# A two-layer chunk-banded attention step on one core: layer B's gates projected with the weights held still, and the softmax sums divided into the probabilities

## The chip, the cores and the metric

The program runs on one core of one Trainium2 chip. The metric is the device time of one execution in microseconds. The kernel before was run three times: median 2267.89 us, lowest 2266.09, highest 2268.76. One further execution was taken with the hardware profiler, and every view of the trace below is of that one.

## What is computed

Two layers of gated attention run over 2048 prompt tokens and 64 sample tokens, model width 1024. The part of the reference that matters here:

```python
def gated_attention_layer(x_p, x_s, ck, cv, norm_g, w_in, q_g, k_g, w_out, ...):
    qp, kp, vp, gp = project(x_p, norm_g, w_in, q_g, k_g, n_heads, n_kv)
    op = prompt_band_attention(qp, kp, vp, past_chunks, bias_fn, sinks)
    y_p = x_p + (op * jax.nn.silu(gp)) @ w_out
```

`project` normalises each token (RMS over 1024), multiplies with one matrix for queries, keys, values and gates, and normalises each head of the queries and keys again. Layer A has 16 query heads over 2 key heads and a window of 128 tokens; layer B has 16 heads of 64 columns with keys of their own and sees its own chunk of 64 tokens and the 8 chunks before. In layer B the probabilities are a plain softmax, `p = exp(s - m) / sum`, the output of a head is `p @ v`, and it is multiplied by `silu(gate)` before the output matrix.

## The kernel before

All products are made in two parts: a tensor is split into a high and a low float32r part, and a product is the sum of three matmuls, high by high, high by low, low by high. TensorE (PE) runs its instructions in the order in which the program is written; the order on ScalarE (ACT), VectorE (DVE), GpSimd (POOL) and on the DMA queue of SyncE (SP) is set by a scheduler.

The work on PE is one long stream. A `Filler` holds all projections as jobs cut in small steps (one step is the three matmuls of one eighth of the model width) and is advanced to a mark between the pieces of the attention; so a projection of a later unit always lies between the scores and the transposes of an earlier one. Layer A's attention comes first, then layer A's output projection as filler, then layer B's attention with its own projections as filler, and at the end what is left of layer B's output projection.

Layer B goes over 8 pairs of heads (`hp`), and for each pair over 8 prompt units of 256 tokens (two tiles of 128) and one sample unit of 64 tokens. For a prompt unit the steps are:

- **Projection** (`project`, lines 489 to 491). For each tile the activations `xx` stand in the array and the 512 columns of weights of the pair move: 128 each of queries, keys, values and gates. That is 8 x 3 matmuls of 512 columns for a tile, 48 for a unit. The result (`pj`, tokens on the partitions) is read by ACT, scaled by the token's inverse norm (`evacuate`, line 512): 384 columns to `pa`, the 128 gate columns to `pb`.
- **Head norms and gate.** DVE and POOL normalise queries and keys (lines 553, 557, 562); ACT makes a tanh of the gates (line 570) and DVE finishes `silu` up to a factor 0.5 (line 571), both for each tile.
- **Queries and keys** (`queries`). PE turns `pa` into `tp`, ACT writes the high parts (lines 1118, 1119), DVE the low parts: two pairs of subtractions and two copies (lines 1123, 1127, 1136).
- **Scores** (`scores`), once for each of the four pairs of tile and head, in the order of the two tiles of one head, then the two of the other. Four matmuls make up to 640 scores per query in `sb` (lines 1174, 1175), DVE adds the bias and takes the extreme in one instruction (line 1178), ACT takes the exponential into `p` and sums it (line 1182). After the last of the four, DVE inverts the four sums at once (line 1188) and POOL multiplies the gates with them into `G` (line 1196).
- **Values** (`values`), one step after its scores: PE transposes `p` (up to five times 128 x 128, line 626), ACT writes the high part `ph` (line 598), DVE the low part `pl` (line 599).
- **Products** (`products`), after the second tile of a head, between and behind the transposes of the next step: `p` by `v` into `o` (line 1264). For the second head of a unit PE also transposes the two tiles of `G` (line 626, `tp<-ident,G`) and ACT copies them, halved, to `gt` (line 1015). `finish_pairs` then adds the parts of `o`, and POOL multiplies with `gt` (line 1026) and stores.

The sample unit goes its own way through `evacuate_sample`, with its gates as tokens on the partitions. A unit's `queries` come in the second of the four steps of the unit before, so the low parts of queries and keys and the scores of the third step meet on DVE. `sb` has two buffers that scores and transposed probabilities share, `p` three, `pj` two.

Of the kernel before, what the change touches and what calls it, by code (L numbers as in the profile page):

```python
# [9 lines left out]
F32 = mybir.dt.float32  # L10
# [40 lines left out]
def hybrid_encoder_kernel(  # L51
# [87 lines left out]
    skew = dr.tile([2, 16, P, VL], F32, tag="skew", name="skew")  # L139

# [332 lines left out]

    def project(tile_, xc, w, C, res, ps=None):
        tt, t0, n = tile_
        ps = ps or psum("pj", 512, 2)
        for k in range(KC):
            wh, wl = weights_of(w, k)
            xh, xl = xc.parts[k // 2]
            if xl is None:  # L480
                if k == 0:
                    nc.tensor.matmul(ps[:, :C], xh[:, k % 2, :], wh, start=True, stop=False)
                nc.tensor.matmul(ps[:n, :C], xh[:, k % 2, :n], wl, start=False, stop=False)
                if k > 0:
                    nc.tensor.matmul(ps[:, :C], xh[:, k % 2, :], wh, start=False, stop=k == KC - 1)
                cost = 2 * C / 2400
            else:
                xh, xl = (a[:, k % 2, t0 : t0 + n] for a in (xh, xl))
                nc.tensor.matmul(ps[:n, :C], xh, wh, start=k == 0, stop=False)  # L489
                nc.tensor.matmul(ps[:n, :C], xh, wl, start=False, stop=False)  # L490
                nc.tensor.matmul(ps[:n, :C], xl, wh, start=False, stop=k == KC - 1)  # L491
                cost = 3 * C / 2400
            if k < KC - 1:
                yield cost
        res.append(ps)
        return cost
# [533 lines left out]
    def layer_b():  # L1030
# [4 lines left out]
        def add_unit(hp, unit):  # L1035
# [7 lines left out]
            def prefetch():  # L1043
                for j in range(NO):
                    assert finished["x1", j] == 2 or j * OT >= u * UT + T
                st.x[hp, u] = x = load_act(x1, u * UT, T, False, T == TS, None, xs[1], hp > 0)
                return x
# [6 lines left out]
            def gen():  # L1054
# [3 lines left out]
                for e, (tt, t0, n) in enumerate(tiles):  # L1058
                    out = []
                    c = yield from project((tt, t0, n), xc, st.w[hp], 512, out)  # L1060
# [11 lines left out]
                    pr = evacuate(1, tt, n, out[0], 512, P, it.gate[:, e])  # L1072
# [3 lines left out]
                    it.todo += head_norm(n, pr[:n, 0:256]) + gate(n, it.gate[:n, e])  # L1076
# [7 lines left out]
                    it.ready = e == len(tiles) - 1  # L1084
                    yield c
# [55 lines left out]
        def scores(it, i, h):  # L1141
# [45 lines left out]
            if c == w - 1:  # L1187
                nc.vector.reciprocal(it.sm[:n, :w], it.sm[:n, :w])
                it.G = G = t("G", [P, 256])
                if u == NU:  # L1190
                    nc.gpsimd.tensor_tensor(
                        G[:, 0:HD], it.gate[:, 0, 0:HD], it.sm[:, 0:1].to_broadcast([P, HD]), op=ALU.mult
                    )
                    return
                for e in range(len(tiles)):
                    nc.gpsimd.tensor_tensor(
                        G[:n, e * P : (e + 1) * P].rearrange("p (h d) -> p h d", d=HD),
                        it.gate[:n, e].rearrange("p (h d) -> p h d", d=HD),
                        it.sm[:n, 2 * e : 2 * e + 2].unsqueeze(2).to_broadcast([n, 2, HD]),
                        op=ALU.mult,  # L1200
                    )
# [51 lines left out]
        def products(it, h):  # L1253
# [18 lines left out]
            def rest():  # L1272
                if h == 1:
                    n = tiles[0][2]
                    GT = psum("tp", 512, 1)
                    for e, (_, t0, _) in enumerate(tiles):
                        transpose(GT[:, t0 : t0 + n], it.G[:n, e * P : (e + 1) * P])
                    gt = gate_t(GT[:, :T].rearrange("p (j s) -> p j s", j=1), T)
# [4 lines left out]
                if h == 1:  # L1283
                    finish_pairs(
                        it.O[:, : 2 * T].rearrange("p (j e s) -> p j e s", j=1, e=2),
                        gt,
# [87 lines left out]
    def block_scales(o):  # L1374
# [4 lines left out]
        sums_to_scales(1, tiles[0], [sums(tt * P, (tt + 1) * P) for tt in tiles], psum("o", 512, 1))  # L1379

# [183 lines left out]
```

## Time and profile before

| what | value |
|---|---|
| median of three runs | 2267.89 us |
| the profiled execution | 2266.69 us, its span 2264.9 us |
| granted TensorE clock | 0.998 |
| busy share of the span: PE, DVE, ACT, POOL | 99%, 69%, 63%, 37% |
| layer B's attention in the span, about | 900 to 2080 us |

The span runs from the first to the last instruction; 1.8 us of the execution lie outside it. Times in the trace are microseconds from the span's start. A row of the timeline gives the start, the duration and the engine, then the line, the operation, the tile written and the tiles read. A matmul's recorded duration holds its whole way through the array, and several are on the way at once; what one of them costs PE in a stream is the distance from its start to the start of the next.

### The profile page before, as it was taken

How to read it: one execution, taken by the hardware profiler on the slowest of the kernel's cores; microseconds unless marked ns; L12 is line 12 of the kernel's file. 1: busy time of each engine (PE TensorE's matmuls, PEld its weight loads, DVE VectorE, ACT ScalarE, POOL GpSimd, SP SyncE). 2: the span in 40 equal slices, each digit the busy share in tenths (PEclk: the TensorE clock that was granted, in tenths of full speed). 3: DMA queues.
4: the chain of work that ended last, by engine and by line, in shares of the span. 5: the costliest groups of instructions: out<-in, count | busy, mean ns of one | idle time of the engine just before them, and what ended most of it. 6: DMA issues, size and time to landing. Idle time of an engine off the chain costs nothing.

```text
span 2264.9 us, 42136 instructions
## 1 busy us (share of the span) xinstructions
PE 2233.4 (99%) x13869; PEld 1965.2 (87%) x13869; DVE 1567.5 (69%) x5184; ACT 1425.0 (63%) x3610; POOL 841.8 (37%) x1196
## 2 busy tenths in 40 slices
PE   8999999999999999999999999999999999999999
PEld 7887888888889998888888888888888888888999
DVE  7889888888785546776776767767767677675211
ACT  6888877777784335766665756656656566566321
POOL 5654533333254456432222322222222222224442
PEclk9999999999999999999999999999999999999999
DMA  8846546754446767454444544544445435444664
GB/s 281 286 137 216 169 140 181 230 175 145 150 133 189 223 194 279 153 192 139 153 144 132 167 136 128 165 144 142 144 138 166 127 120 177 133 128 119 201 184 140
DMA packets 232285, 379.35 MB, mean 167 GB/s; under 512 B 24753, under 2 KB 163393, under 8 KB 232033
## 3 DMA queue, kind: packets, MB, share of 16 engines
q1 hardware_dynamic: 232064, 376.65, 53.8%
q8 instruction: 109, 1.79, 0.3%
q14 instruction: 112, 0.91, 0.1%
HBM read 296.13 MB, written 82.08 MB: 167 GB/s over the span
## 4 chain that ended last, share of the span: by engine, by line
PE 84%; DVE 5%; ACT 5%; issue 3%; DMA 2%; POOL 1%; SPq 0%; ACTq 0%; POOLq 0%; DVEq 0%
PE pj L489 14%; PE pj L491 14%; PE pj L490 14%; PE o L1264 6%; PE sb L626 6%; PE pj L1418 5%; PE pj L1419 4%; PE pj L1420 4%; PE tp L626 3%; PE sb L1175 3%; PE sb L1174 3%; PE sa L626 2%; PE o L971 1%; PE sa L917 1%; PE sa L918 1%
## 5 line engine op out<-in xcount | busy, mean ns | idle before, releaser
L489 PE MATMUL pj<-wh,xx 128*128 128x512 f32 (+1 forms) x1648 | 660.7, 401 | 1.6 <-ACT pb L512 0.9
L490 PE MATMUL pj<-wl,xx 128*128 128x512 f32 (+1 forms) x1648 | 636.5, 386 | 3.1 <-DVE wl L317 3.1
L491 PE MATMUL pj<-wh,xx 128*128 128x512 f32 (+1 forms) x1648 | 637.7, 387 | 0.0
L491 PEld LDWEIGHTS pj<-wh,xx 128*128 128x128 f32 x1648 | 310.2, 188 | 67.6 <-POOL xx L388 0.2
L489 PEld LDWEIGHTS pj<-wh,xx 128*128 128x128 f32 x1648 | 311.0, 189 | 43.1 <-ACT pb L512 1.6
L490 PEld LDWEIGHTS pj<-wl,xx 128*128 128x128 f32 x1648 | 311.5, 189 | 41.4 <-DVE wl L317 3.5
L1182 ACT ACTIVATE p<-p,nm 128x640 f32<-128x640 f32 (+5 forms) x264 | 200.0, 757 | 231.4 <-DVE nm L1178 230.5
L388 POOL TENSOR_TENSOR xx<-xraw,xx 128x528 fp32r<-128x528 f32 (+1 forms) x200 | 266.4, 1355 | 174.8 <-ACT xx L387 155.1
L557 POOL TENSOR_TENSOR f<-f,mhalf 128x4 f32<-128x4 f32 (+3 forms) x221 | 226.8, 1027 | 213.0 <-DVE f L553 204.1
L599 DVE TENSOR_TENSOR pl<-sb,ph 128x640 fp32r<-128x640 f32 (+4 forms) x264 | 193.4, 733 | 151.5 <-ACT ph L598 150.3
L1418 PE MATMUL pj<-xx,wh 128*128 128x264 f32 x1024 | 293.5, 287 | 0.2 <-DVE res L1423 0.2
L1419 PE MATMUL pj<-xx,wh 128*128 128x264 f32 x1024 | 291.4, 285 | 0.2 <-POOL xx L388 0.2
L1420 PE MATMUL pj<-xx,wl 128*128 128x264 f32 x1024 | 289.9, 283 | 0.0
L1178 DVE CUSTOM_DVE_ANT_0 p<-sb,BT 128x640 f32<-128x640 f32 (+5 forms) x272 | 197.0, 724 | 78.1 <-PE sb L1175 66.2
L1026 POOL TENSOR_TENSOR o<-gt,o 128x256 f32<-128x256 f32 (+1 forms) x132 | 103.5, 784 | 376.6 <-ACT p L934 105.5
L626 PE MATMUL sb<-ident,p 128*128 128x128 f32 x1144 | 213.3, 280 | 3.4 <-ACT sq L570 1.1
L387 ACT CAST xx<-xraw 128x528 fp32r<-128x528 f32 (+1 forms) x200 | 121.3, 627 | 142.6 <-PE pj L1420 126.7
L598 ACT CAST ph<-sb 128x640 fp32r<-128x640 f32 (+4 forms) x264 | 162.9, 617 | 63.1 <-PE sb L626 59.5
L1418 PEld LDWEIGHTS pj<-xx,wh 128*128 128x128 f32 x1024 | 192.8, 188 | 0.9 <-DVE res L1423 0.4
L1419 PEld LDWEIGHTS pj<-xx,wh 128*128 128x128 f32 x1024 | 192.4, 188 | 0.6 <-POOL xx L388 0.4
L1420 PEld LDWEIGHTS pj<-xx,wl 128*128 128x128 f32 x1024 | 192.6, 188 | 0.0
L1423 DVE TENSOR_TENSOR res<-pj,res 128x264 f32<-128x264 f32 x128 | 55.0, 430 | 190.7 <-PE pj L1420 184.0
(212 smaller groups left out, 4815.2 us busy)
## 6 DMA issues: line engine op xcount, KB each, us to landing
xx<-xsb SPq DMA_DIRECT2D x224, 512.0 KB, 4.2
xx<-xsa SPq DMA_DIRECT2D x88, 512.0 KB, 4.7
xraw<-oga SPq DMA_DIRECT2D x64, 264.0 KB, 3.5
xraw<-ogb SPq DMA_DIRECT2D x64, 264.0 KB, 3.4
xsa<-xx SPq DMA_DIRECT2D x32, 512.0 KB, 4.4
wraw<-in_w_in_b_dram SPq DMA_DIRECT2D x64, 256.0 KB, 3.1
xsb<-xx SPq DMA_DIRECT2D x32, 512.0 KB, 4.9
xraw<-in_x_dram SPq DMA_DIRECT2D x40, 256.0 KB, 4.0
```

The lines of the kernel that those rows point to most:

```text
L388: nc.gpsimd.tensor_tensor(xl, rv, xh.bitcast(F32), op=ALU.subtract)
L489: nc.tensor.matmul(ps[:n, :C], xh, wh, start=k == 0, stop=False)
L490: nc.tensor.matmul(ps[:n, :C], xh, wl, start=False, stop=False)
L491: nc.tensor.matmul(ps[:n, :C], xl, wh, start=False, stop=k == KC - 1)
L557: nc.gpsimd.tensor_tensor(fv, fv, mhalf[:n, :H], op=ALU.pow)
L599: b = nc.vector.tensor_tensor(dst_lo, src, dst_hi.bitcast(F32), op=ALU.subtract)
L626: nc.tensor.transpose(out, in_, ident[:n, :n])
L1178: mi = nc.vector.tensor_tensor_reduce(out=p[r, :nk], in0=S[r, o : o + nk], in1=b, op0=ALU.add, op1=ALU.min, scale=1.0, scalar=3e38, accum_ ...
L1182: ex = nc.scalar.activation(p[:n, :nk], p[:n, :nk], AF.Exp, scale=-1.0, bias=it.nm[:n, c : c + 1], accum_out=it.sm[:n, c : c + 1],)
L1418: nc.tensor.matmul(ps[:, :OT], wh, oh, start=k == 0, stop=False)
L1419: nc.tensor.matmul(ps[:, :OT], wh, ol, start=False, stop=False)
L1420: nc.tensor.matmul(ps[:, :OT], wl, oh, start=False, stop=k == KC - 1)
```

## The change

Three things change for the prompt units of layer B; layer A and the sample units keep their arithmetic.

1. `project` now makes 384 columns (queries, keys, values) for each tile. The gates come in a third pass over the same weights and activations, `project_turned`: the 128 gate columns of the weights stand in the array and the 256 tokens of the unit move. The result has the gate columns on the partitions and the tokens along the row.
2. In that layout the inverse norm of a token is a number for each column. It is written to DRAM once per tile (`rows_b`), and for each unit spread over the partitions by a DMA (`rb`, 128 KB). DVE multiplies it in while it reads `pj`, ACT makes one tanh of 128 x 256, DVE finishes. `finish_pairs` takes the gates as they are: the transposes of `G`, the copy to `gt` and the products on POOL are gone.
3. The inverse sums go into the probabilities: for each of the four pairs of tile and head DVE inverts one sum, and ACT multiplies `p` by it in place, ahead of the transposes.

```diff
+    def project_turned(xc, w, C, T, res):
+        ps = psum("pj", 512, 2)
+        for k in range(KC):
+            wh, wl = (a[:, C : C + P] for a in weights_of(w, k))
+            xh, xl = (a[:, k % 2, :T] for a in xc.parts[k // 2])
+            nc.tensor.matmul(ps[:, :T], wh, xh, start=k == 0, stop=False)
+            nc.tensor.matmul(ps[:, :T], wh, xl, start=False, stop=False)
+            nc.tensor.matmul(ps[:, :T], wl, xh, start=False, stop=k == KC - 1)
...
@@ layer_b, prefetch
+                if not last:
+                    it.row = t("rb", [P, UT])
+                    load(it.row, rows_b[u].partition_broadcast(P))
@@ layer_b, gen
-                    c = yield from project((tt, t0, n), xc, st.w[hp], 512, out)
+                    c = yield from project((tt, t0, n), xc, st.w[hp], 512 if last else 384, out)
...
-                    pr = evacuate(1, tt, n, out[0], 512, P, it.gate[:, e])
+                    pr = evacuate(1, tt, n, out[0], 384, 0)
...
-                    it.todo += head_norm(n, pr[:n, 0:256]) + gate(n, it.gate[:n, e])
+                    it.todo += head_norm(n, pr[:n, 0:256])
...
+                    c = yield from project_turned(xc, st.w[hp], 384, T, out)
+                    g = it.gate.rearrange("p a b -> p (a b)")
+                    nc.vector.scalar_tensor_tensor(g, out[0][:, :T], 0.5, it.row, op0=ALU.mult, op1=ALU.mult)
+                    e = t("sq", [P, 256], 2)
+                    nc.scalar.activation(e, g, AF.Tanh)
+                    nc.vector.scalar_tensor_tensor(g, e, 1.0, g, op0=ALU.add, op1=ALU.mult)
@@ scores
-            if c == w - 1:
-                nc.vector.reciprocal(it.sm[:n, :w], it.sm[:n, :w])
+            nc.vector.reciprocal(it.sm[:n, c : c + 1], it.sm[:n, c : c + 1])
...
-                for e in range(len(tiles)):
-                    nc.gpsimd.tensor_tensor(
-                        G[:n, e * P : (e + 1) * P].rearrange("p (h d) -> p h d", d=HD),
...
+            else:
+                nc.scalar.activation(p[:n, :nk], p[:n, :nk], AF.Identity, scale=it.sm[:n, c : c + 1])
@@ products
-                if h == 1:
-                    n = tiles[0][2]
-                    GT = psum("tp", 512, 1)
-                    for e, (_, t0, _) in enumerate(tiles):
-                        transpose(GT[:, t0 : t0 + n], it.G[:n, e * P : (e + 1) * P])
-                    gt = gate_t(GT[:, :T].rearrange("p (j s) -> p j s", j=1), T)
...
-                        gt,
+                        it.gate.rearrange("p a b -> p (a b)").unsqueeze(1),
@@ block_scales
+        for tt in tiles:
+            if tt < NT:
+                store(rows_b[tt // 2][tt % 2 * P : (tt % 2 + 1) * P].rearrange("(p o) -> p o", o=1), rr[1][:, tt : tt + 1])
```

Below, the order in which instructions stand on their engines, in the unit with tokens 512 to 767 of the fifth head pair; lines of after are 10 to 40 higher for the same code. First the PE of before where the projection passes from one tile to the next: `pj` is the projection's result, `wh` and `wl` the weights' parts, `xx` the activations, `sb` the scores.

```order
L489 MATMUL pj_19807<-wh_18859,xx_19616 128x512
L490 MATMUL pj_19807<-wl_18860,xx_19616 128x512
L491 MATMUL pj_19807<-wh_18859,xx_19616 128x512
L1174 MATMUL sb_19881<-KA,q_3978_19774 128x384
L1175 MATMUL sb_19881<-KA,q_1_102 128x384
L1174 MATMUL sb_19881<-KA,q_3978_19774 128x256
L1175 MATMUL sb_19881<-KA,q_1_102 128x256
L489 MATMUL pj_19900<-wh_18384,xx_19610 128x512
```

The PE of after where the projection passes from the second tile to the turned pass:

```order
L503 MATMUL pj_20705<-wh_19582,xx_20427 128x384
L504 MATMUL pj_20705<-wl_19583,xx_20427 128x384
L505 MATMUL pj_20705<-wh_19582,xx_20427 128x384
L480 MATMUL pj_20771<-xx_20421,wh_19076 128x256
L481 MATMUL pj_20771<-xx_20421,wh_19076 128x256
L482 MATMUL pj_20771<-xx_20421,wl_19077 128x256
```

A tile's steps move 384 columns in place of 512, and a third result of 8 x 3 steps of 256 columns follows, in which the activations are what moves. Next the PE of before at the products that end a unit: `ident,p` are transposes of probabilities, `ident,G` those of the gates, `o` the products.

```order
L626 MATMUL sb_19936<-ident,p_19882 128x128
L1264 MATMUL o_19855<-ph_19851,VT 128x256
L1264 MATMUL o_19855<-ph_19851,VT 128x128
L626 MATMUL sb_19936<-ident,p_19882 128x128
L1264 MATMUL o_19855<-pl_19852,VT 128x128
L626 MATMUL sb_19936<-ident,p_19882 128x128 x3
L626 MATMUL tp_19947<-ident,G_19842 128x128 x2
L1264 MATMUL o_19855<-pl_19852,VT 128x256
```

The same place of after:

```order
L640 MATMUL sb_20777<-ident,p_20712 128x128
L1283 MATMUL o_20682<-ph_20678,VT 128x256
L1283 MATMUL o_20682<-ph_20678,VT 128x128
L640 MATMUL sb_20777<-ident,p_20712 128x128
L1283 MATMUL o_20682<-pl_20679,VT 128x128
L640 MATMUL sb_20777<-ident,p_20712 128x128 x3
L1283 MATMUL o_20682<-pl_20679,VT 128x256
```

Only the two transposes of `G` are gone. Last the DVE of before behind the third scores of that unit: line 1136 copies and lines 1123 and 1127 make the low parts of the next unit's queries and keys, line 562 ends its head norm, line 599 is the low part of the transposed probabilities of the step before, line 1178 the next bias and extreme.

```order
L1136 CAST q_4018_19980<-q_4018_19980 64x256
L1123 SCALAR_TENSOR_TENSOR q_0_101<-tp_19975,qsc,q_4018_19980 64x256
L1127 SCALAR_TENSOR_TENSOR KA<-tp_19975,ksc,KA 64x256
L562 TENSOR_TENSOR pa_19970<-pa_19970,f_19994 128x256
L599 TENSOR_TENSOR pl_19935<-sb_20020,ph_19934 128x5x128
L1123 SCALAR_TENSOR_TENSOR q_0_101<-tp_19975,qsc,q_4018_19980 64x256
L1127 SCALAR_TENSOR_TENSOR KB<-tp_19975,ksc,KB 64x256
L1136 CAST q_4018_19980<-q_4018_19980 64x256
L571 SCALAR_TENSOR_TENSOR pb_19806<-sq_20031,pb_19806 128x128
L1178 ISA p_20041,nm_19880<-sb_20040,BT 128x640
```

The DVE of after behind the third scores of the same unit, from their own bias and extreme on; line 1107 reads the turned gates, line 1213 inverts a sum:

```order
L1204 ISA p_20831,nm_20710<-sb_20830,BT 128x640
L1204 ISA nm_20710 128x1
L1162 CAST q_3956_20825<-q_3956_20825 64x256 x2
L576 TENSOR_TENSOR pa_20767<-pa_20767,f_20789 128x256
L1107 SCALAR_TENSOR_TENSOR pb_20641<-pj_20771,rb_20429 128x256
L1149 SCALAR_TENSOR_TENSOR q_0_109<-tp_20820,qsc,q_3956_20825 64x256
L1153 SCALAR_TENSOR_TENSOR KA<-tp_20820,ksc,KA 64x256
L1149 SCALAR_TENSOR_TENSOR q_0_109<-tp_20820,qsc,q_3956_20825 64x256
L1153 SCALAR_TENSOR_TENSOR KB<-tp_20820,ksc,KB 64x256
L1213 RECIPROCAL sm_20709<-sm_20709 128x1
L613 TENSOR_TENSOR pl_20776<-sb_20874,ph_20775 128x5x128
L1110 SCALAR_TENSOR_TENSOR pb_20641<-sq_20856,pb_20641 128x256
```

The inversion of the third sum stands behind the copies, the head norm's end, the reading of the turned gates and all four low parts, and the low part of the step before now stands behind it. In 30 heads of full width (640 scores) the inversion stands behind all four low parts, and in 19 of these behind lines 576 and 1107 too.

## Prediction on record

> **What bounds the kernel now.** I read the page first, for the engine that sets the end. Of its chain of waits this is the share by engine:
>
> ```profile
> PE 84%; DVE 5%; ACT 5%; issue 3%; DMA 2%; POOL 1%; SPq 0%; ACTq 0%; POOLq 0%; DVEq 0%
> ```
>
> TensorE carries it. Next the table by stretches over layer B's attention (1060 to 2040 us, five stretches), of which the sum shows whether any other engine is near its limit there; then the table of what PE waited for in 1060 to 2060 us, its two largest entries:
>
> ```profile
> sum 980.00, PE 977.53 PEld 843.86 DVE 698.29 ACT 620.40 POOL 270.29; mean PE 195.51 PEld 168.77 DVE 139.66 ACT 124.08 POOL 54.06
> ```
>
> ```profile
> PE sb L626 <- ACT sq L570: 1.1, 3, 0.4
> PE tp L626 <- ACT gt L1015: 1.1, 1, 1.1
> ```
>
> PE is busy 977.5 of 980 us, and its longest waits sum to about 1 us each; DVE is at 71%, ACT at 63%. So in this stage a microsecond of instructions taken from PE's stream or put into it is a microsecond of the run, and the other engines matter only where they make PE wait. What a matmul costs in the stream is read as the distance between starts, from PE's timeline of two units:
>
> ```profile
> 1701.37 0.39 PE L489 MATMUL pj<-wh,xx 128*128 128x512 f32 x1
> ...
> 1702.52 0.39 PE L491 MATMUL pj<-wh,xx 128*128 128x512 f32 x1
> ...
> 1704.70 0.34 PE L1174 MATMUL sb<-KB,q 128*128 128x384 f32 x1
> 1704.87 0.34 PE L1175 MATMUL sb<-KB,q 128*128 128x384 f32 x1
> 1705.05 0.28 PE L1174 MATMUL sb<-KB,q 128*128 128x256 f32 x1
> 1705.17 0.28 PE L1175 MATMUL sb<-KB,q 128*128 128x256 f32 x1
> 1705.29 0.40 PE L489 MATMUL pj<-wh,xx 128*128 128x512 f32 x1
> ...
> 1707.56 0.29 PE L626 MATMUL sb<-ident,p 128*128 128x128 f32 x1
> 1707.61 0.37 PE L1264 MATMUL o<-pl,VT 128*128 128x256 f32 x1
> ...
> 1716.55 0.30 PE L626 MATMUL sb<-ident,p 128*128 128x128 f32 x1
> 1716.68 0.38 PE L626 MATMUL tp<-ident,G 128*128 128x128 f32 x2
> 1716.82 0.37 PE L1264 MATMUL o<-pl,VT 128*128 128x256 f32 x1
> 1717.02 0.28 PE L1264 MATMUL o<-ph,VT 128*128 128x256 f32 x1
> ...
> 1717.73 0.39 PE L489 MATMUL pj<-wh,xx 128*128 128x512 f32 x1
> ```
>
> Five distances of 512 columns take 1.15 us (1701.37 to 1702.52), so 0.230 to 0.232 us each; two of 384 take 0.35, so 0.175; six of 256 columns 0.71 (1717.02 to 1717.73), so 0.118. From a transpose to the next product are 0.05 us without the gates' transposes (1707.56) and 0.27 us with them (1716.55).
>
> **The change part by part.** There are 64 prompt units (8 head pairs, 8 units); each term is for one, then times 64.
>
> *The projection.* Before: 48 x 0.232 = 11.14 us. After: 48 x 0.175 + 24 x 0.118 = 8.40 + 2.83 = 11.23 us. The columns are the same; 24 more starts cost 0.096 us, times 64 = **+6.1 us**, all on the path. With 0.230 for the wide one and 0.120 (1705.05 to 1705.29) for the narrow it would be +15, with 0.174 and 0.117 +1.5; I take the longer measurements, +6.
>
> *The gates' transposes.* Two leave each unit: 0.27 - 0.05 = 0.22 us, times 64 = **-14.1 us**, on the path. The bounds are 0.13 (two starts, if the other 0.09 is a change of mode that stays) and 0.27. With them go the copy to `gt` and its hold on `tp`, of which the waits show 1.1 us.
>
> *POOL, and the gates' way.* POOL loses two products per unit and gains nothing. ACT loses two readings of gate columns, two tanh of 128 columns and the copy, DVE two finishing instructions; ACT gets one tanh of 256 columns, DVE a reading of `pj` and one finish. Nobody waits for these before the unit's last products, a whole unit later; cost zero. If the reading of `pj` came late PE would wait for a result buffer, but it has the whole first tile of the next unit, 24 x 0.175 = 4.2 us and what lies between, until the buffer is needed.
>
> *Row loads and stores.* 64 loads of 128 KB and 16 stores are added on SP. A row is fetched at the prefetch and read at the end of the unit after; what stands behind a waiting load on SP are activation and weight loads with a similar lead. The activations are also held longer: the first quarter of a unit's is now free at 81% of the unit's projection (two tiles and a quarter of the third pass, 9.1 of 11.23 us) where it was 62%, and the last load of the next unit, which takes that place, is needed at 28% of its own. The lead falls from 66% to 47%, still 5.3 us of projection alone. Zero, with up to 3 us kept for the ends of head pairs.
>
> *The probabilities.* Four inversions and four scalings per unit now stand between the exponential and the transposes. Three rows price them on DVE (the normalisation, the low part and the inversion in 1060 to 2060 us), one on ACT; scaling is not in the trace, and the exponential of the same shape, in place, is its nearest row.
>
> ```profile
> L562 DVE TENSOR_TENSOR pa<-pa,f 128x256 f32<-128x256 f32 x105 | 51.0, 486 | 16.2 <-POOL f L557 15.2
> L1123 DVE SCALAR_TENSOR_TENSOR q<-tp,qsc,q 64x256 fp32r<-64x256 f32 x104 | 50.3, 483 | 4.9 <-ACT KB L1119 2.4
> ...
> L1188 DVE RECIPROCAL sm<-sm 128x4 f32<-128x4 f32 x53 | 9.4, 177 | 25.5 <-ACT p L1182 25.4
> ```
>
> ```profile
> L1182 ACT ACTIVATE p<-p,nm 128x640 f32<-128x640 f32 x162 | 134.6, 831 | 150.2 <-DVE nm L1178 149.7
> ```
>
> As load this fits: the wide scalings add at most another 134.6 us to ACT's 620 of 980, before anything is taken off, so under 79%. What counts is the delay. The timeline of a third head, DVE, PE and ACT:
>
> ```profile
> 1719.66 0.82 DVE L1178 CUSTOM_DVE_ANT_0 p<-sb,BT 128x640 f32<-128x640 f32 x1
> 1720.41 0.08 DVE L1178 DVE_READ_ACCUMULATOR2_ANT nm<- 128x1 f32 x1
> 1720.52 0.59 DVE L1136 CAST q<-q 64x256 fp32r<-64x256 f32 x2
> 1721.12 0.48 DVE L1123 SCALAR_TENSOR_TENSOR q<-tp,qsc,q 64x256 fp32r<-64x256 f32 x1
> ...
> 1723.17 0.82 DVE L599 TENSOR_TENSOR pl<-sb,ph 128x640 fp32r<-128x640 f32 x1
> ```
>
> ```profile
> 1718.79 0.42 PE L1174 MATMUL sb<-KB,q 128*128 128x384 f32 x1
> ...
> 1724.05 0.33 PE L626 MATMUL sb<-ident,p 128*128 128x128 f32 x1
> ```
>
> ```profile
> 1720.77 0.83 ACT L1182 ACTIVATE p<-p,nm 128x640 f32<-128x640 f32 x1
> ```
>
> The exponential ends at 1721.6 and the transposes come at 1724.05: 2.45 us of slack. An inversion and a scaling done at once need 0.18 + 0.83, so most heads have room. Not this one: by the order of after, its inversion stands behind both copies, the head norm's end, the reading of the turned gates and all four low parts. From the first score matmul: 0.87 to the bias (1718.79 to 1719.66), 0.86 to the copies, 0.60 for them, 0.49 for the norm, 0.48 for the gates (row L1123, also from PSUM), 2.05 for the four low parts (1721.12 to 1723.17), 0.18 inversion, 0.83 scaling: 6.36 us, and some 0.1 of hand-over (1720.41 + 0.08 to 1720.77 holds one with a queue). PE's own way to those transposes in after's order: the scores 0.59, 9 turned matmuls 1.06, 18 of 384 columns 3.15, five transposes at 0.11 (the two of `G`, 0.22) 0.55, four more scores 0.59, and 0.17 for two returns from transposes (1716.82 to 1717.02 is 0.20 against 0.118): 6.11 us. So PE waits about 0.35 us, once in each of the 30 full-width heads that stand so: **+10.5 us**. From below it is nothing, if the norm or the copies end sooner; from above it is 0.6 us for all 44 heads with four low parts ahead, the 14 narrower ones too: 26 us.
>
> **Sum.** +6.1 - 14.1 + 10.5 = +2.5 us. On the profiled execution's 2266.69 us that is 2269.2; its time lies 1.2 below the median of the three runs, 2267.89, so I forecast **2270.4 us**. A measurement of this kernel can tell about 0.2%, 4.5 us, from no change: 2263.4 to 2272.4.
>
> **The rivals.**
>
> *The slack holds.* If the third heads' chain is 0.35 us shorter than I count, PE never waits and its stream alone remains: 6.1 - 14.1 = -8, so 2260. For it: PE's waits are nearly nil today. Against it: after's order puts 5 us of DVE work behind one bias.
>
> *The inversion on DVE takes over.* Everything that waits for the inversion in DVE's queue, the low part of the step before first of all, is late too, and PE waits 0.6 us in all 44 heads: -8 + 26 = +18, so 2286. It decides from 0.7 us of delay on, since the low part is then also late for the products between the transposes. For it: DVE is at 71% and gets 0.8 us more per unit (three inversions of 0.18, one gate reading of 0.48, less than 0.2 taken off). Against it: POOL and ACT lose work at the same place.
>
> *A price for each matmul.* 1536 more matmuls, each with its own load of weights, which the page gives as
>
> ```profile
> L491 PEld LDWEIGHTS pj<-wh,xx 128*128 128x128 f32 x1648 | 310.2, 188 | 67.6 <-POOL xx L388 0.2
> ```
>
> If loads came one after another, a narrow matmul would cost 0.188 in place of 0.118: 1536 x 0.07 = 108 us, so 2378. Against it stand the six distances of 0.118, each with such a load. The Trainium skill, "TensorE: Matmul & The Clock Gate", section "Back-to-back issue gap", speaks against the change in the same way: a stream of load and matmul pairs sustains about 81 ns at 128 columns and 131 ns at 512, which is much start and little column. By a straight line through these a unit would go from 48 x 131 to 48 x 114 + 24 x 98 ns, an estimate of +1.5 us a unit or +98 us in all. The trace has 232, 175 and 118 ns, nearly in the ratio of the columns, and decides.
>
> *A transpose costs its whole duration.* The groups of PE give
>
> ```profile
> L626 PE MATMUL tp<-ident,G 128*128 128x128 f32 x256 | 49.5, 275 | 0.0
> ```
>
> At 0.275 the 128 transposes would be worth 35 us, and the sum -35 + 6 + 10.5 = -18.5, so 2249. The starts, 0.22 us for two, speak against it. The Trainium skill, the same page, section "Part 4: PE-mode transpose", gives about 275 ns in one kernel's context; the duration agrees with this row, but as a price in a stream it would make the sum -18.5, and the starts do not bear it out.
>
> *The transposes were in shadow.* If PE waits at the end of a unit for `pl` anyway, taking `G` away returns nothing: +6 + 10.5, so 2284. One such wait would have to recur in every unit, and the waits table has none.
>
> **How the numbers follow.** No measurable change, 0.38, likeliest for the narrow sum of terms of both signs; its own range is 2263 to 2273. The slack holds 0.25, the full transpose 0.02: faster 0.27. DVE takes over 0.28, in shadow 0.04, a price for each matmul 0.03: slower 0.35. The range reaches from 2258 (the first rival with the transposes at their upper bound of 0.27) to 2287 (the second with a microsecond); outside are the price for each matmul, the full transpose and the far ends, under 2 in 10.
>
> **What would show it.** In the profile after: starts 0.175 apart in the 384-column projection and 0.118 in the turned pass; no `tp<-ident,G` in layer B; inversions on DVE directly ahead of scalings; and, for the third heads, transposes that begin right behind the scaling, with the table of waits naming ACT's `p` as PE's releaser some 30 times at about 0.35 us. I am wrong if PE's waits in this stage stay under 3 us (then 2260), if they exceed 20 us or name DVE's `pl` (then the second rival), or if the turned pass's starts lie further apart than 0.13.

## The result, and the profile after

The changed kernel takes 2337.5 us (median of 5 runs) where the kernel before takes 2267.9: a ratio of 1.0321, interval 1.0307 to 1.0336. It is 70 us slower, forecast was +2.5 and at most +19. The profiled execution of after took 2346.5 us (span 2344.7, mean granted clock 0.988; before 0.998), 9 us above the median. The ratios and intervals leave out two executions, one of 5627.6 us among the four of e5 and one of 4379.8 us among the ten of e14, which the medians of these two kernels still count.

The chain of waits, by engine, and the sum over the same five stretches of layer B (1060 to 2040 us) as before:

```profile
PE 69%; DVE 13%; DMA 8%; ACT 6%; issue 3%; SPq 1%; POOL 0%; DVEq 0%; ACTq 0%; POOLq 0%
```

```profile
sum 980.00, PE 957.92 PEld 935.31 DVE 708.40 ACT 698.23 POOL 222.64; mean PE 191.58 PEld 187.06 DVE 141.68 ACT 139.65 POOL 44.53
```

TensorE's share of the chain fell from 84 to 69%; VectorE and DMA took it. In layer B TensorE lost 20 of 980 us. What it waited for, in the two places where the waits lie, first 1060 to 2060 us (layer B), then 760 to 940 us (the second half of layer A's output projection and the first unit of layer B); us in total, times, longest:

```profile
PE sb L640 <- DVE pl L613: 14.3, 22, 1.2
PE sb L640 <- ACT p L1220: 8.1, 13, 3.6
```

```profile
PE pj L1434 <- DVE res L1439: 19.3, 7, 4.8
PE o L442 <- DVE BT L1385: 5.9, 1, 5.9
PE pj L503 <- DVE res L1439: 2.4, 1, 2.4
```

Two losses, then. The second stands where I had put none: from the first output-projection matmul to the last, layer A's took 237.7 us, 207.6 before; and of the waits of the second table, those for `res` come to 0.2 us before. The starts are as forecast, one matmul of 384 columns 0.18 us, three of the turned pass, 256 columns, 0.35:

```profile
1505.70 0.34 PE L505 MATMUL pj<-wh,xx 128*128 128x384 f32 x1
1505.88 0.28 PE L480 MATMUL pj<-xx,wh 128*128 128x256 f32 x1
...
1508.09 0.28 PE L480 MATMUL pj<-xx,wh 128*128 128x256 f32 x1
...
1508.44 0.28 PE L480 MATMUL pj<-xx,wh 128*128 128x256 f32 x1
```

To separate the steady state from the rest I use the time of one **head pair**: the start of the sample unit's second projection matmul in the fourth pair and in the eighth, and a quarter of the distance between the two. Before and after:

```profile
1418.23 0.39 PE L483 MATMUL pj<-wl,xx 128*64 128x512 f32 x1
...
2025.07 0.39 PE L483 MATMUL pj<-wl,xx 128*64 128x512 f32 x1
```

```profile
1484.41 0.40 PE L497 MATMUL pj<-wl,xx 128*64 128x512 f32 x1
...
2102.82 0.40 PE L497 MATMUL pj<-wl,xx 128*64 128x512 f32 x1
```

151.71 us a pair before, 154.60 after: +2.89, over 8 pairs 23 us of the 70. The forecast's terms make +0.3 a pair.

### The profile page after: what moved, and what is told of

It reads as the page before. It is cut to its first block, busy times and chain, and to the rows that moved or that the text cites. A ratio compares the mean times of both kernels' runs of the same rounds, so it can differ in the third digit from the quotient of the medians.

```text
span 2344.7 us, 45395 instructions
## 1 busy us (share of the span) xinstructions
PE 2255.8 (96%) x15277; PEld 2121.7 (90%) x15277; DVE 1602.1 (68%) x5376; ACT 1546.5 (66%) x3610; POOL 789.9 (34%) x1068
## 4 chain that ended last, share of the span: by engine, by line
PE 69%; DVE 13%; DMA 8%; ACT 6%; issue 3%; SPq 1%; POOL 0%; DVEq 0%; ACTq 0%; POOLq 0%
PE pj L503 10%; PE pj L505 10%; PE pj L504 10%; PE o L1283 5%; PE sb L640 5%; PE pj L1434 4%; PE pj L1435 4%; PE pj L1436 4%; DMA x<-res 3%; PE sb L1201 2%; PE sb L1200 2%; PE sa L640 2%; DVE q L1149 2%; PE tp L640 2%; PE pj L480 1%
## 5 line engine op out<-in xcount | busy, mean ns | idle before, releaser
L503 PE MATMUL pj<-wh,xx 128*128 128x384 f32 (+2 forms) x1648 | 603.7, 366 | 5.4 <-ACT pb L526 2.8
L504 PE MATMUL pj<-wl,xx 128*128 128x384 f32 (+2 forms) x1648 | 580.9, 353 | 2.9 <-DVE wl L318 2.9
L505 PE MATMUL pj<-wh,xx 128*128 128x384 f32 (+2 forms) x1648 | 582.1, 353 | 0.0
L1434 PE MATMUL pj<-xx,wh 128*128 128x264 f32 x1024 | 298.4, 291 | 19.9 <-DVE res L1439 19.8
L1435 PE MATMUL pj<-xx,wh 128*128 128x264 f32 x1024 | 295.7, 289 | 0.7 <-POOL xx L389 0.7
L613 DVE TENSOR_TENSOR pl<-sb,ph 128x640 fp32r<-128x640 f32 (+4 forms) x264 | 193.7, 734 | 87.8 <-ACT ph L612 86.1
L1220 ACT ACTIVATE p<-p,sm 128x640 f32<-128x640 f32 (+4 forms) x256 | 195.2, 763 | 61.7 <-DVE sm L1213 60.4
L592 POOL TENSOR_TENSOR VT<-pa,VT 128x128 fp32r<-128x128 f32 x144 | 68.7, 478 | 465.7 <-ACT VT L591 463.6
L1434 PEld LDWEIGHTS pj<-xx,wh 128*128 128x128 f32 x1024 | 197.3, 193 | 21.4 <-DVE res L1439 20.8
L1435 PEld LDWEIGHTS pj<-xx,wh 128*128 128x128 f32 x1024 | 197.1, 193 | 1.1 <-POOL xx L389 0.9
L640 PEld LDWEIGHTS sb<-ident,p 128*128 128x128 f32 x1144 | 147.5, 141 | 55.4 <-ACT p L1220 41.2
```

Source lines behind the costliest of these rows:

```text
L640: nc.tensor.transpose(out, in_, ident[:n, :n])
L1220: nc.scalar.activation(p[:n, :nk], p[:n, :nk], AF.Identity, scale=it.sm[:n, c : c + 1])
L1434: nc.tensor.matmul(ps[:, :OT], wh, oh, start=k == 0, stop=False)
L1435: nc.tensor.matmul(ps[:, :OT], wh, ol, start=False, stop=False)
```

## The row stores

**What the trace shows.** In 760 to 940 us SyncE's queue waited for this (after, then before):

```profile
SPq L1403 <- DMA x<-res: 68.9, 15, 8.2
```

```profile
SPq L1387 <- DMA x<-res: 29.5, 15, 4.0
```

The residual's load needs the buffer that a store of layer A's output still reads, and that store now lands late. The DMA issues of one such place, 781 to 791 us (KB each, median us from issue to landing), and what the queues moved in 40 slices of it:

```profile
GB/s 34 144 127 287 368 283 292 346 368 380 360 213 48 17 0 0 0 0 0 0 0 0 66 0 0 0 0 0 0 0 0 0 0 0 0 0 0 0 33 0
...
x<-res SPq DMA_DIRECT2D x1, 264.0 KB, 9.5
...
rowb<-rms SPq DMA_DIRECT2D x2, 0.5 KB, 9.0
```

Two stores of half a KB take 9 us, the store of 264 KB issued just ahead of them 9.5 (the median of these stores before, in 760 to 1000 us, is 3.8), and for more than half of that time the queues move next to nothing. Four experiments asked whether this is the loss, and whose.

**The stores alone, on the kernel before.**

```diff
+        for tt in tiles:
+            if tt < NT:
+                store(rows_b[tt // 2][...], rr[1][:, tt : tt + 1])
```

> The kernel before with one thing added: the 16 stores of the row scales, 128 elements of 4 bytes each, at the place where after has them; nothing reads them, the gates are as before. Theory A (the row stores make the residual's loads late in layer A's output projection, and that is about 30 us of the loss, with some more at the start of layer B): 2293 to 2306 us. Theory B (the loss comes from the scaling of the probabilities alone, and what the profile of after shows in the output projection comes from the 64 row loads or the turned pass): 2266 to 2272 us.

Measured: 2299.7 us, ratio 1.0143 (1.0126 to 1.0161). Theory A, in the middle of its range.

**After without the stores** (gates without the norm's scale).

```diff
-                store(rows_b[tt // 2][...], rr[1][:, tt : tt + 1])
...
-                    load(it.row, rows_b[u].partition_broadcast(P))
+                    load(it.row, x1[0, 0, u * UT : u * UT + UT].partition_broadcast(P))
```

> After without the 16 row stores; the row loads stay and read a row of layer A's output in their place, so the gates lack the norm's scale. Theory A: the output projection falls back from 237.7 us to about 208, and the time by 30 to 45 us, to 2292 to 2307; what stays above the kernel before is the chain of the probabilities. Theory B: 2330 to 2340.

Measured: 2301.5 us, 1.0152 (1.0136 to 1.0168): 36 us less than after, with all 64 row loads still there.

**After with contiguous rows.**

```diff
+    def block_row(u):
+        ps = psum("o", 512, 1)
+        transpose(ps[0:2, 0:P], rr[1][:, 2 * u : 2 * u + 2])
+        rw = t("o1", [P, 256])[:, 0:P]
+        nc.vector.tensor_copy(rw[0:2], ps[0:2, 0:P])
+        store(rows_b[u].rearrange("(a p) -> a p", a=2), rw[0:2])
```

> After with the rows made contiguous before the store: one transpose on TensorE per block of 256 tokens, some 2 us after the scales, a copy on VectorE, and one store of 2 x 512 bytes where two stores of 128 x 4 bytes were. Same result as the reference. Theory A with the cost in the 4-byte elements: as without the stores, plus 1 to 3 us for 8 transposes and their waits, 2293 to 2309. If any store behind the residual's stores is to blame, whatever its shape: 2325 to 2340.

Measured: 2302.9 us, 1.0157 (1.0139 to 1.0176). The same bytes in the same queue, 512 in a piece, cost 1.4 us against none at all. The output projection takes 208.9 us.

**The stores on another queue.**

```diff
-                store(rows_b[tt // 2][...], rr[1][:, tt : tt + 1])
+                nc.scalar.dma_start(rows_b[tt // 2][...], rr[1][:, tt : tt + 1])
```

> After with the 16 row stores, still 4 bytes an element, issued from ScalarE's queue in place of SyncE's. If the loss is order in SyncE's queue (the stores stand there and hold what is behind them): the time falls by 25 us or more, to 2295 to 2312. If it is in the transfers themselves (the 4-byte elements hold up the landing of the stores around them, whichever queue issued them): no more than 8 us better, 2329 to 2340.

Measured: 2343.5 us, 1.0339 (1.0322 to 1.0356), nothing gained and a little above the second range. So it is not the order in SyncE's queue, but the transfers.

**Spaced elements, on the kernel before** (asked last, together with the last runs of the next section).

```diff
-    rows_b = [dr.tile([UT], F32, ...) for u in range(NU)]
+    rows_b = [dr.tile([UT, P], F32, ...) for u in range(NU)]
...
+                store(rows_b[tt // 2][tt % 2 * P : (tt % 2 + 1) * P, 0:1], rr[1][:, tt : tt + 1])
```

> The kernel before with the 16 stores of 128 elements of 4 bytes, as measured at 2299.7 us, but each element into a line of its own, 512 bytes from the next; nothing reads them. If the elements hold each other up because neighbours lie in one line of memory: 2266 to 2278. If each 4-byte element has its price wherever it goes: 2290 to 2306.

Measured: 2265.2 us, 0.9996 (0.9986 to 1.0005), just under the first range: nothing is left of the cost. The view of the row tile gives the landing times of the 16 stores, min, median and max in us, packed (the first of these kernels) and spaced:

```profile
DMA to landing us min/median/max: 7.6/8.9/11.1
```

```profile
DMA to landing us min/median/max: 1.8/3.0/5.5
```

The same number of 4-byte elements costs nothing that can be measured when each has 512 bytes to itself. The Trainium skill, "DMA: Bandwidth & Descriptors", section "Specifications", says that below 512 bytes a DMA engine reads, modifies and writes. Taken as a price for each small piece this trace does not bear it out, since the spaced pieces are as small; it fits pieces that modify the same 512 bytes and must take turns, which the runs suggest and do not prove: the spaced elements of a store also lie in 64 KB of memory in place of 512 bytes.

## The probabilities and the gates

With the row stores out of the way 2302.9 us are left, 35 above before. The trace shows the step of the forecast as it was drawn. A third head in after, VectorE, ScalarE and TensorE:

```profile
1756.79 0.49 DVE L1153 SCALAR_TENSOR_TENSOR KB<-tp,ksc,KB 64x256 fp32r<-64x256 f32 x1
1757.31 0.16 DVE L1213 RECIPROCAL sm<-sm 128x1 f32<-128x1 f32 x1
1757.51 0.82 DVE L613 TENSOR_TENSOR pl<-sb,ph 128x640 fp32r<-128x640 f32 x1
1758.25 0.41 DVE L1110 SCALAR_TENSOR_TENSOR pb<-sq,pb 128x256 f32<-128x256 f32 x1
...
1760.40 0.17 DVE L1213 RECIPROCAL sm<-sm 128x1 f32<-128x1 f32 x1 [0.99 <-ACT p L1208]
```

```profile
1757.51 0.83 ACT L1220 ACTIVATE p<-p,sm 128x640 f32<-128x640 f32 x1 [1.55 <-DVE sm L1213]
```

```profile
1758.48 0.30 PE L640 MATMUL sb<-ident,p 128*128 128x128 f32 x1 [0.41 <-ACT p L1220]
```

The inversion follows the last low part of the queries and keys, the scaling follows at once, TensorE waits 0.41 us. The last VectorE row shows the other side: the next inversion stands at the head of VectorE's queue and idles 0.99 us until the exponential is done, with a low part behind it. Summed over 1060 to 2060 us, after and before:

```profile
DVE sm L1213 <- ACT p L1208: 96.6, 118, 1.8
```

```profile
DVE sm L1188 <- ACT p L1182: 25.4, 39, 1.0
```

Theory C says that this wait in VectorE's queue is what costs, theory D that the scaling on ScalarE does. Four runs on the kernel with contiguous rows; the first three leave out the division by the sums.

```diff
# e5: neither
-            nc.vector.reciprocal(it.sm[:n, c : c + 1], it.sm[:n, c : c + 1])
...
-                nc.scalar.activation(p[:n, :nk], p[:n, :nk], AF.Identity, scale=it.sm[:n, c : c + 1])
# e6: the inversion only
-                nc.scalar.activation(p[:n, :nk], p[:n, :nk], AF.Identity, scale=it.sm[:n, c : c + 1])
# e7: the scaling only
-            nc.vector.reciprocal(it.sm[:n, c : c + 1], it.sm[:n, c : c + 1])
# e8: whole computation
-            nc.vector.reciprocal(it.sm[:n, c : c + 1], it.sm[:n, c : c + 1])
+            nc.gpsimd.tensor_tensor(it.sm[:n, c : c + 1], it.sm[:n, c : c + 1], mone[:n], op=ALU.pow)
```

> After with contiguous rows (the kernel measured at 2302.9 us), without the inversion of the prompt heads' sums and without the scaling of their probabilities; the division by the sums is left out. What remains of the change is the turned projection, the gates' way and the absence of the gates' transposes. By the prediction's own terms (+6.1 and -14.1 us) and 1 to 3 us for the rows: 2259 to 2264 us. If the turned pass or its matmuls cost more than was counted: 2270 or more.

> As the kernel without both, with the four inversions per unit on VectorE put back, each right behind its exponential in the program, and still no scaling (the division is left out). Theory C (the inversion stands in VectorE's queue, waits there for ScalarE's exponential and holds up the low parts behind it): VectorE's wait for the exponential stays near 100 us and half or more of the 33 us of TensorE's waits come back, those named for the low parts: 2275 to 2290. Theory D (the scaling's 0.83 us on ScalarE is the cost): 2259 to 2266, as without both.

> As the kernel without both, with the scaling of the probabilities on ScalarE put back, by the sums themselves in place of their inverses (the division is left out), so that ScalarE has the whole work and VectorE none. Theory C: no wait of TensorE's beyond the kernel without both by more than 5 us: 2259 to 2268. Theory D: 2290 to 2305.

> After with contiguous rows and the whole computation, the four inversions per unit as a power of -1 on GpSimd in place of VectorE's reciprocals. Theory C: VectorE's wait for the exponential goes, and with it the waits for the low parts; the scalings wait for GpSimd (some 0.5 to 0.7 us an inversion, by its 0.70 us for 128x2): 2262 to 2280. Theory D: 2295 to 2310, since ScalarE's scaling is as long and no earlier.

Measured: neither 2282.1 us, 1.0065 (1.0048 to 1.0082); inversion only 2286.9, 1.0089 (1.0069 to 1.0110); scaling only 2289.2, 1.0102 (1.0085 to 1.0118); inversion on GpSimd 2291.3, 1.0116 (1.0098 to 1.0135). The first missed: without inversion and scaling the kernel still is 0.65%, 14.7 us, above before, which put the forecasts for the others off by that floor. Against the floor, inversion and scaling cost about 5 and 8 us alone (the interval of the first overlaps the floor's; the steady pairs below are clearer), and together 1.0157 - 1.0065 = 0.92%, 20.9 us. In steady pairs they nearly add: +0.77, +0.59, both +1.49 us (table below). So neither C nor D alone; GpSimd's inversions save 11.6 of the 20.9 us.

**On the kernel before**, the scaled probabilities alone, with its own gates:

```diff
-            if c == w - 1:
-                nc.vector.reciprocal(it.sm[:n, :w], it.sm[:n, :w])
+            nc.vector.reciprocal(it.sm[:n, c : c + 1], it.sm[:n, c : c + 1])
...
+                nc.scalar.activation(p[:n, :nk], p[:n, :nk], AF.Identity, scale=it.sm[:n, c : c + 1])
...
-                        transpose(GT[:, t0 : t0 + n], it.G[:n, e * P : (e + 1) * P])
+                        transpose(GT[:, t0 : t0 + n], it.gate[:n, e])
```

> The kernel before with its last part of the change alone: each head's sum inverted on VectorE behind its exponential, the probabilities scaled in place on ScalarE, the gates left as they are, projected and transposed as before. Theory C+D (the inversion in VectorE's queue and the scaling cost about the same in either layout, 21 us by the difference of the two kernels with contiguous rows): 2284 to 2292. If they cost much only behind the turned gates' instructions: 2269 to 2277.

Measured: 2285.4 us, 1.0081 (1.0066 to 1.0096), +18 us: much the same price in either layout.

**The floor.** What is left of the change without the division is the turned pass and the gates' way. TensorE's waits of the kernel with neither, 1060 to 2060 us, in which the low part of the step before is still named:

```profile
PE sb L640 <- DVE pl L613: 10.9, 19, 1.2
```

One such wait in that kernel, VectorE and TensorE; its gates' reading of the PSUM buffer is L1109, their finish L1112:

```profile
1559.57 0.42 DVE L1109 SCALAR_TENSOR_TENSOR pb<-pj,rb 128x256 f32<-128x256 f32 x1
1559.91 0.47 DVE L1151 SCALAR_TENSOR_TENSOR q<-tp,qsc,q 64x256 fp32r<-64x256 f32 x1
...
1561.39 0.49 DVE L1155 SCALAR_TENSOR_TENSOR KB<-tp,ksc,KB 64x256 fp32r<-64x256 f32 x1
1561.91 0.43 DVE L1112 SCALAR_TENSOR_TENSOR pb<-sq,pb 128x256 f32<-128x256 f32 x1
1562.37 0.82 DVE L613 TENSOR_TENSOR pl<-sb,ph 128x640 fp32r<-128x640 f32 x1
```

```profile
1563.25 0.33 PE L640 MATMUL sb<-ident,p 128*128 128x128 f32 x1 [0.30 <-DVE pl L613]
```

Both gate instructions and the four low parts of queries and keys stand in VectorE's queue ahead of the low part (L613) that frees the buffer for TensorE's transposes. Theory E puts the floor down to the gates' instructions, theory F to TensorE's own stream.

```diff
# e9: no gate work (a constant tile multiplies); e13: nor row loads and stores
-                    nc.vector.scalar_tensor_tensor(g, out[0][:, :T], 0.5, it.row, op0=ALU.mult, op1=ALU.mult)
-                    e = t("sq", [P, 256], 2)
-                    nc.scalar.activation(e, g, AF.Tanh)
-                    nc.vector.scalar_tensor_tensor(g, e, 1.0, g, op0=ALU.add, op1=ALU.mult)
# e10, e11: tanh and finish in begin() of the second head's products
+                    nc.scalar.activation(e, g, AF.Tanh)
+                    nc.gpsimd.tensor_tensor(e, e, g, op=ALU.mult)
+                    nc.gpsimd.tensor_tensor(g, e, g, op=ALU.add)
# e14, e15: project_turned and the gate work ahead of the two tiles' project
```

> The kernel with contiguous rows and neither inversion nor scaling (2282.1 us measured, 0.65% above the kernel before), now also without the turned gates' three instructions behind the projection: VectorE's reading of the PSUM buffer, ScalarE's tanh, VectorE's finish. GpSimd multiplies by a constant tile of the same size; the turned pass stays on TensorE. Theory E (these instructions, in VectorE's queue ahead of the low parts, are what keeps the kernel without the division above the one before): TensorE's waits for the low parts fall from 13.4 to under 4 us: 2264 to 2271. Theory F (TensorE's own stream with its narrower matmuls costs it): 2277 to 2284, waits as before.

> The same kernel with the gate work, but the tanh and the finish moved to the second head's first product a unit later, and the finish from VectorE to GpSimd (a product and a sum); VectorE keeps the reading of the PSUM buffer alone. Theory E: about half of what the kernel without gate work gains, 2270 to 2277. Theory F: 2279 to 2285.

> The whole computation: contiguous rows, inversions on GpSimd (2291.3 us measured), and the late tanh and finish on GpSimd. Theory E: 5 to 12 us less than that kernel, 2279 to 2286; still above the kernel before, since the reading of the PSUM buffer and the scalings stay. Theory F: 2289 to 2295, or more, if GpSimd's queue delays the inversions.

Measured: no gate work 2291.8 us, 1.0114 (1.0099 to 1.0129), slower, against both theories; late gate 2275.4, 1.0038 (1.0024 to 1.0053), as E has it; with the whole computation 2290.5, 1.0104 (1.0087 to 1.0120), no gain. The trace of the first points at its row loads. Nothing reads them there, so in SyncE's queue they wait for each other (first row, 960 to 1010 us), and near 980 us a weight load came so late that ScalarE waited 11.5 us for it (second row) and TensorE stood for 10.4:

```profile
SPq L1063 <- DMA rb<-rowb: 17.9, 12, 2.4
```

```profile
ACT wh L315 <- DMA wraw<-in_w_in_b_dram: 13.8, 2, 11.5
```

Its steady pairs take 150.87 us, less than before. In the whole computation, ScalarE's waits for GpSimd's inversions rose from 29.8 to 49.0 us when the finish went to GpSimd too. TensorE's waits for `pl` in 1060 to 2060 us fell from 12.5 to 7.1 us, and those for `p` rose from 0.9 to 6.2: what one gained the other took. So the question was asked again.

> The kernel without gate work and without the division once more, now also without the 64 row loads that nothing read there and without the row stores: TensorE's whole new stream with nothing behind the turned pass. Theory E, cleaned: a head pair takes 150.9 us as in that kernel's steady pairs (151.7 before), the 10 us stall and the late start go, and the run takes 2258 to 2266 us, 0 to 0.4% under the kernel before. Theory F: 2277 or more.

> Contiguous rows, neither inversion nor scaling (2282.1 us; 153.1 us a head pair), with the turned pass at the head of each unit's projection in place of its end, so that the three gate instructions fall into another step than the four low parts of queries and keys. If the gate work costs by its place, ahead of the low part that TensorE waits for: 150.9 to 152 us a pair and 2266 to 2275. If it costs by its amount on VectorE: 153 us a pair and 2279 to 2285.

> The whole computation: contiguous rows, inversions on GpSimd (2291.3 us; 153.5 us a pair), turned pass first. By place: 8 to 16 us less, 2275 to 2284. By amount: 2288 to 2294.

Measured: without gate work and rows 2265.1 us, 0.9991 (0.9982 to 1.0001), 27 us less than with the unread row loads, which had cost 14.6 us ahead of the first pair's mark and 14.4 in the second pair (by the profiled executions); turned pass first 2269.1, 1.0012 (1.0002 to 1.0023); the whole computation with inversions on GpSimd and the turned pass first 2280.4, 1.0060 (1.0045 to 1.0075). Theory E, and by place: the same pass and gate work a step away from the four low parts cost 1.0012 + 0.0009 = 0.21%, 5 us, where they cost 1.0065 + 0.0009 = 0.74%, 17 us. TensorE's waits in 1060 to 2060 us for the low part, 10.9 us in 19 times above, are 2.7 us in the first of the three kernels and 4.2 us in the second, which has a new wait beside it, for a result buffer that VectorE reads (`pb`, the gates of the sample unit):

```profile
PE sb L639 <- DVE pl L612: 2.7, 7, 0.6
```

```profile
PE pj L503 <- DVE pb L550: 4.3, 5, 0.9
PE sb L640 <- DVE pl L613: 4.2, 5, 1.8
```

The head pairs of the first, for 151.71 before:

```profile
1417.16 0.39 PE L496 MATMUL pj<-wl,xx 128*64 128x512 f32 x1
...
2020.72 0.40 PE L496 MATMUL pj<-wl,xx 128*64 128x512 f32 x1
```

That is 150.89 us. All head pairs, read from the same two rows of each trace (the six rows of the table from e14 to "after" have the 64 row loads too, and all but the last of these the contiguous stores; e15 has both):

| kernel | us a pair | ratio of the run |
|---|---|---|
| before | 151.71 | 1 |
| stream alone (e13) | 150.89 | 0.9991 |
| + gates first in the unit (e14) | 151.42 | 1.0012 |
| + gates, finish late on GpSimd (e10) | 152.22 | 1.0038 |
| + gates where the change has them (e5) | 153.09 | 1.0065 |
| + inversion (e6) / + scaling (e7) | 153.86 / 153.68 | 1.0089 / 1.0102 |
| + both (e3) | 154.58 | 1.0157 |
| after, with its row stores | 154.60 | 1.0321 |
| before, scaled probabilities (e12) | 154.07 | 1.0081 |
| whole, best of these (e15) | 152.77 | 1.0060 |

No version tried with the whole computation beats the kernel before, and the stream alone, with the gate work, the rows and the division all left out, is 0.09% under it, within what the measurement can tell.

## Why the prediction was wrong

*The sum of the loss.* From the ratios, in us of 2267: stream -2, gates' way in its place 17, inversion and scaling 21, row stores 37 (1.0321 - 1.0157). Together 73; forecast -8, 0, +10.5 and 0. So two terms put at zero, the row stores and the gates' way, make 54 of the 73, and the term of the probabilities was half of what it cost.

*"Row loads and stores ... Zero, with up to 3 us kept for the ends of head pairs."* The largest failure. The working follows the loads through SyncE's queue; of the stores it says only that they are 16. They carry 8 KB in 2048 pieces, land after 9.1 us (median), and delay the stores beside them, for which the residual's loads wait; the working asks about none of this. The loads have no run of their own, but e14 has all 64 and lies 5 us above e13, which has none and no gate work either, so where they are read they cost 5 us at most.

*"POOL, and the gates' way ... Nobody waits for these before the unit's last products, a whole unit later; cost zero."* True of the gates, and wrong of what stands behind them. Two VectorE instructions of 0.42 and 0.43 us at the projection's end lie ahead of the low part for which TensorE's next transposes wait. The forecast counted the first of them in the third head's chain (0.48 us ahead of the inversion) and nowhere else. Runs e13 against e5 give 17 us, the rows of e5 included, and e14 shows that the place costs 12 of them.

*"The probabilities ... PE waits about 0.35 us, once in each of the 30 full-width heads."* The wait is real, 0.41 us at the head shown, but it is only half of the mechanism, and the term was mis-sized. In steady pairs both parts cost 1.49 us, over 8 pairs 11.9 for 10.5, and that nearness is luck: over four steady pairs of the kernel with contiguous rows TensorE waits for `p` only 8 times, 2.9 us in all, where the forecast has 15 waits and 5.2 us; the other half comes through `pl`, 10.4 us against 7.0 in the kernel with neither, which the forecast had left to a rival. The whole run lost 20.9; the other 9 lie at the start of layer B, where pairs two and three of the kernel with contiguous rows take 152.6 and 159.0 us and of the one with neither 149.0 and 151.1. In pair three TensorE is idle for 6.7 us against 0.8, with one wait of 3.6 us for `p`, and just behind that wait its granted clock is 0.83 in 1130 to 1140 us. Why these two pairs are so exposed stays open.

*The rival "the inversion on DVE takes over"* named ACT's and DVE's waits in all 44 heads, 26 us. With contiguous rows the table of waits has 45 such waits (21 for `p`, 24 for `pl`) and 33 us. Its count and size held, though whether the waits fall in those 44 heads is not shown; its cause held only in part, since 21 waits for `pl` (13.4 us) remain with no inversion at all. *"The slack holds"* fell with TensorE's 22 us of waits. *"A price for each matmul"* and the two transpose rivals are ruled out by the starts of 0.12 and 0.18 us and by the stream's -0.82 us a pair (forecast -1.0). The stream's two terms were near: from start to start, with waits taken off, the projection takes 1.2 us a pair more in e13 than before (forecast 0.8) and the transposes 1.8 less (1.8). The -0.82 us over 8 pairs would be -6.6; the ratio of the whole run gives -2 (-4 to 0).

Two figures of the working come out otherwise by its own terms, and nothing hung on them: with 0.27 us for the transposes the range's low end is 2257, not 2258, and the loads' lead before is 75%, not 66%, since the last load was needed at 6 of 16 steps, 37.5%.

## What to carry to other kernels

Price a store by its pieces and where they fall, not by its bytes alone: here stores of 128 elements of 4 bytes, packed into 512 bytes of memory, took 9 us to land and made the store just ahead of them as late; a transpose to two rows of 512 bytes, or elements 512 bytes apart, took the cost away. Work whose own result nobody awaits can still have a price through what stands behind it in its engine's queue (17 us here): ask what that is, and move the work a step before giving it up (5 us). And an instruction that waits for another engine's last result, as the inversion does for its exponential, is better kept out of the queue of the engine that feeds the busiest one; moving it to GpSimd saved 11.6 us here.

## What the runs showed of the hardware

Besides the packed stores: when TensorE stood for some us its granted clock fell, and it paid again. It stood for 3.58 us until 795.02 us, for one, and the clock is 0.51 in 794 to 795 and 0.50 in 795 to 800 us. The whole stretch of 780 to 920 us in after (busy time and count of PE, PEld, DVE, ACT, POOL; granted clock, DMA share, GB/s):

```profile
780.00:920.00 140.00, 112.30 (x771) 111.19 (x770) 45.85 (x98) 33.62 (x60) 52.39 (x53) 0.89 0.56 155
```

Before, the clock there is 1.00. Where it fell it stood at 0.50, so 0.89 over 140 us is 31 us at half, an estimate, and of the 30 us that the output projection lost up to 15 are clock rather than wait. The Trainium skill, "TensorE: Matmul & The Clock Gate", section "Part 1: The HAM clock gate (the "warmup" mystery)", describes a gate that passes half of the pulses until TensorE has been busy for about 3.4 us; the trace agrees, in seven half-clock stretches of 3.4 or 6.8 us there.
